# A recurrence that centres v in its transposing product and sums over head channels by one fp32 product

## The chip, the core and the metric

The kernel runs on one core of one Trainium2 chip. The metric is the device time of one execution in microseconds; three runs gave 1673.81, 1668.88 and 1673.68 us, with a median of 1673.68. All other times here come from one profiled execution, which took 1675.3 us and whose span from the first to the last instruction is 1673.2 us. Names of engines: PE is TensorE (PEld its weight loads), DVE is VectorE, ACT is ScalarE, POOL is GpSimd, SP is SyncE, whose queue issues most DMAs.

## The reference

One block of a hybrid transformer, with 1024 positions of width 1024: a normalised and modulated input, a token mixer of two branches (attention with forget gates, and an RWKV7 recurrence, each with 8 heads of 64 channels), a gated merge of both, and a feed-forward part with a short convolution. Only the recurrence is changed. Its core, cut to what matters:

```
kk = heads(k * k_k)
kk = kk / jnp.maximum(jnp.sqrt(jnp.sum(kk * kk, axis=-1, keepdims=True)), L2_EPS)
...
def step(state, inp):
    r_t, w_t, k_t, v_t, a_t, b_t = inp
    sa = jnp.einsum('bhvk,bhk->bhv', state, a_t)
    state = state * w_t[:, :, None, :] + sa[..., None] * b_t[:, :, None, :] + v_t[..., None] * k_t[:, :, None, :]
    y_t = jnp.einsum('bhvk,bhk->bhv', state, r_t)
    return state, y_t
...
mean = jnp.mean(y, axis=-1, keepdims=True)
var = jnp.mean(jnp.square(y - mean), axis=-1, keepdims=True)
y = ((y - mean) * lax.rsqrt(var + GN_EPS)).reshape(bsz, seq, RWKV_WIDTH) * ln_w + ln_b
bonus = (jnp.sum(r_h * k_h * r_k, axis=-1, keepdims=True) * v_h).reshape(bsz, seq, RWKV_WIDTH)
return ((y + bonus) * g).astype(p.dtype)
```

Four sums run over the 64 channels of a head: of kk squared, of r k r_k, of y (its mean) and of the squared, centred y (its variance). Since y is linear in v along the channels of v, a v whose mean over these channels is zero gives a y whose mean is zero.

## The kernel before

The kernel works channel-major: the 128 partitions hold the channels of two heads, the free axis 512 positions. Large products are made of three fp32r products each (high x high, high x low and low x high halves of the operands), 24 matrix products of 128x512 for one output tile of a 1024-deep contraction.

Stages of the profiled execution: modulation and start (0 to about 55 us), the first projections and the lora chain (to 149), the recurrence (149 to 627), attention (627 to 839), the branch products br (839 to about 905), and the output product and feed-forward part (to the end).

The recurrence goes through eight units (p, hf): a pair of heads p (0 to 3) and a half hf of the positions, in the order (0,0), (0,1), (1,0) and so on. For each unit

- `pre` makes ssq (the sum of kk squared), decays, keys and scores, transposes v and a scaled a to position-major tiles vt and at (4 transposes each, copied to UV by ACT and to QA by DVE), transposes keys (tb), forms q from scores and UV, the sum bs and with it bon, the bonus, on DVE;
- `inverse` inverts triangular 32x32 blocks on DVE, by 62 small instructions (t and E, L740 and L744 before, L732 and L736 after); the result E goes through DRAM (DMAs se, then TT) into TT;
- `main` transposes TT to X on DVE (L881), and TensorE makes from X and TT in turn xi, zi and uw, and then eight chunks of sp and yp, where sp updates the state S (L941) and yp is the output. The rest of `main` takes y from PSUM, subtracts its mean, divides by its deviation, applies ln_w, ln_b and the bonus, and stores o.

The next unit's `pre` runs beside a unit's `main`. Before the change a helper, `head_sums`, makes each sum over head channels: ACT casts the operand to fp32r (hi), POOL subtracts (lo), and TensorE multiplies both by blk_r, a matrix of two 64x64 blocks of ones.

What sets the order: TensorE's order is written out by a planner, `Weave`. Each chain of work is a generator; `weave.now` advances by the planned cost of each product (`mm_cost`), a chain yields the planned nanoseconds until it can go on, and in between the planner takes single products from a queue of large ones: r, k, v and q, k projections (ps_rkv, qk), the position-major v, and at last 16 gates (gt; 48 products each). What is left of the queue when the recurrence ends is used up in attention, where a gate runs in one PSUM buffer, rk_ps, as a late gate: 24 products for a half, then Abs and Relu on ACT read rk_ps, then Exp, Ln, an addition on DVE, Exp and a store to d_gate (`gate_out`, L1186). `drain` ends attention only when no gate is pending. Behind it `br_open` casts and splits the first weights of the branch products (hi_br, L1242). In the recurrence the other engines' orders come from a scheduler; in attention DVE's and ACT's are the order of the code.

Attention's heads are loaded by POOL's queue (`load_head`: stA, stB, vh), and SP's queue issues the stores of the gates.

## Time and profile before

| what | from where | value |
|---|---|---|
| time | median of three runs | 1673.68 us |
| profiled execution | its own time; its span | 1675.3 us; 1673.2 us |
| granted TensorE clock | mean over the span | 0.986 |
| recurrence, 149 to 627 us | PE, DVE, ACT, POOL busy | 472.75, 348.22, 215.57, 62.98 us |
| attention, 627 to 839 us | PE, DVE, ACT, POOL busy | 199.57, 163.32, 140.16, 50.43 us |
| sums over head channels | POOL subtractions L727, four groups of eight | 11.7 + 11.4 + 10.4 + 10.4 us |
| granted clock of attention | mean, 627 to 839 us | 0.97 |

How to read it: busy times of several engines overlap, so they are not added; an engine that is busy for nearly the whole of a stage sets that stage's time. In the rows shown below, a group of instructions has its line, engine, operation, output<-inputs and count, then busy us and the mean ns of one, then the idle time before them with what ended it; a timeline row has start and duration in us; a row of waits has the total, the times and the longest. A row of a window has its length, then busy us of PE, PEld, DVE, ACT and POOL, the granted clock as a share of full speed, the DMA share and GB/s. A matmul's recorded duration contains its way through the array; what one costs in a row of them is the distance from start to start.

### The profile page before, as it was taken

To read this page: it belongs to the slowest core of one execution; us is meant where nothing else is said; L and a number is where in the kernel's file an instruction comes from. 1 tells how busy PE (TensorE), PEld (TensorE's weight loads), DVE (VectorE), ACT (ScalarE), POOL (GpSimd) and SP (SyncE) were. 2 spreads that over 40 slices of the span, in tenths; PEclk is the share of its full clock that TensorE was granted. 3 is DMA by queue.
4 is the path that set the end of the run, shared out by engine and by line. 5 is a ranking of instruction groups with operands and counts; after the bars stand their busy time and mean duration, and the time that the engine had idled before them with its cause. 6 is when DMAs were issued, how large, how long until landed. Compare 5 with 4: busy or idle time off the path is not lost.

```text
span 1673.2 us, 26056 instructions
## 1 busy us (share of the span) xinstructions
PE 1622.3 (97%) x9772; PEld 1333.2 (80%) x9772; DVE 1227.8 (73%) x2390; ACT 808.3 (48%) x1482; POOL 147.8 (9%) x175
## 2 busy tenths in 40 slices
PE   5899999999999998999999999999999999999998
PEld 4677877787977777888878888888888888888886
DVE  5786787888876635888778445897777777786677
ACT  5453343434455545767623244654444444455455
POOL 0010101111111012322022000000000000000000
PEclk8899999999999999999999999999999999999999
DMA  8497744433343236433197420143223323574463
GB/s 333 133 327 213 194 124 130 129 102 113 96 127 92 80 112 155 127 113 119 36 344 264 164 89 39 63 131 108 102 95 99 116 95 108 190 274 154 129 210 107
DMA packets 120974, 239.85 MB, mean 143 GB/s; under 512 B 39888, under 2 KB 48336, under 8 KB 120848
## 3 DMA queue, kind: packets, MB, share of 16 engines
q1 hardware_dynamic: 112896, 220.94, 40.8%
q0 software_dynamic: 7952, 17.25, 3.9%
q8 instruction: 77, 1.26, 0.3%
q14 instruction: 49, 0.40, 0.1%
HBM read 172.59 MB, written 65.54 MB: 142 GB/s over the span
## 4 chain that ended last, share of the span: by engine, by line
PE 82%; DVE 9%; DMA 4%; ACT 3%; issue 2%; SPq 1%; POOL 0%; DVEq 0%; ACTq 0%
PE X L144 13%; PE D L144 13%; PE Y L144 6%; PE gt L144 6%; PE ps_rkv L144 6%; PE wo L144 5%; PE br L144 5%; PE rk_ps L144 4%; PE W L144 3%; PE v L144 2%; PE lg L144 2%; PE ov L144 2%; PE tp L151 2%; PE qk L144 2%; PE low L144 1%
## 5 line engine op out<-in xcount | busy, mean ns | idle before, releaser
L144 PE MATMUL D<-op,op 128*128 128x512 f32 x924 | 209.8, 389 | 0.0
L144 PEld LDWEIGHTS D<-op,op 128*128 128x128 f32 x924 | 173.3, 188 | 36.3 <-DVE op L1269 0.3
L144 PE MATMUL X<-T_m,S 128*128 128x512 f32 x440 | 107.2, 390 | 0.1
L144 PEld LDWEIGHTS X<-T_m,S 128*128 128x128 f32 x440 | 82.4, 188 | 18.2 <-ACT T_m L1694 0.5
L1268 ACT CAST op<-g 128x512 fp32r<-128x512 f32 x77 | 47.8, 621 | 73.8 <-PE D L144 47.9
L1269 DVE TENSOR_TENSOR op<-g,op 128x512 fp32r<-128x512 f32 x77 | 53.0, 688 | 41.5 <-ACT op L1268 41.5
L1505 DVE SCALAR_TENSOR_TENSOR c<-ab,vec,c 128x512 f32<-128x512 f32 x88 | 65.8, 749 | 19.5 <-ACT c L1508 17.9
L1469 DVE TENSOR_TENSOR S<-ur,S 128x512 fp32r<-128x512 f32 x66 | 45.5, 691 | 35.9 <-ACT S L1465 35.7
L270 DVE TENSOR_TENSOR lo_in<-raw_in,hi_in 128x512 fp32r<-128x512 f32 x84 | 57.9, 727 | 14.0 <-PE gt L144 5.0
L1465 ACT CAST S<-ur 128x512 fp32r<-128x512 f32 x66 | 41.0, 622 | 55.8 <-DVE ur L1458 30.9
L1469 DVE TENSOR_TENSOR A<-ur,A 128x512 fp32r<-128x512 f32 x64 | 44.0, 687 | 30.9 <-ACT A L1465 30.7
L268 ACT CAST hi_in<-raw_in 128x1024 fp32r<-128x1024 f32 x42 | 43.9, 1048 | 44.4 <-PE ps_rkv L144 26.6
L740 DVE TENSOR_TENSOR t<-E,M 128x60 f32<-128x60 f32 (+24 forms) x248 | 56.0, 226 | 12.0 <-DMA M<-sm 5.7
L144 PE MATMUL Y<-T_h,A 128*128 128x512 f32 x264 | 63.5, 389 | 0.0
L144 PE MATMUL Y<-T_h,S 128*128 128x512 f32 x264 | 63.3, 389 | 0.0
L744 DVE TENSOR_TENSOR E<-E,t 128x60 f32<-128x60 f32 (+24 forms) x248 | 56.8, 229 | 5.8
L144 PE MATMUL X<-B_b,A 128*128 128x512 f32 x252 | 60.8, 390 | 0.0
L144 PE MATMUL W<-B_f,A 128*128 128x512 f32 x252 | 60.6, 389 | 0.0
L1090 ACT ACTIVATE P<-lg,nm 128x896 f32<-128x896 f32 (+3 forms) x64 | 47.4, 743 | 22.8 <-DVE nm L1086 22.6
L144 PEld LDWEIGHTS Y<-T_h,A 128*128 128x128 f32 x264 | 49.5, 188 | 10.4
L144 PEld LDWEIGHTS Y<-T_h,S 128*128 128x128 f32 x264 | 49.5, 188 | 10.3
L1465 ACT CAST A<-ur 128x512 fp32r<-128x512 f32 x64 | 39.8, 623 | 34.1 <-PE X L144 29.4
(473 smaller groups left out, 4151.9 us busy)
## 6 DMA issues: line engine op xcount, KB each, us to landing
raw_in<-in_w_in SPq DMA_DIRECT2D x50, 512.0 KB, 4.3
wm<-in_w_mod SPq DMA_DIRECT2D x48, 512.0 KB, 7.4
ur<-in_w_up SPq DMA_DIRECT2D x44, 512.0 KB, 4.3
g<-d_g SPq DMA_DIRECT2D x35, 512.0 KB, 3.9
d_g<-gs SPq DMA_DIRECT2D x44, 256.0 KB, 2.0
d_g<-c SPq DMA_DIRECT2D x33, 256.0 KB, 4.6
d_st<-qh SPq DMA_DIRECT2D x64, 128.0 KB, 2.4
d_gate<-gs SPq DMA_DIRECT2D x32, 256.0 KB, 2.7
```

The costliest lines, as they stand in the source:

```text
L144: weave.last = nc.tensor.matmul(o, lhsT, rhs, start=start, stop=stop, skip_group_check=more)
L151: nc.tensor.transpose(o, i, eye)
L268: nc.scalar.copy(hi, raw)
L270: nc.vector.tensor_tensor(lo[:, c : c + NH], raw[:, c : c + NH], f32(hi[:, c : c + NH]), op=ALU.subtract)
L740: i = tt(tv, E32[:, 0:J, s : s + 1].to_broadcast([128, J, W]), M32[:, s : s + 1, s + 1 : 32].to_broadcast([128, J, W]), op=ALU.mult)
L744: tt(E32[:, 0:J, s + 1 : 32], E32[:, 0:J, s + 1 : 32], tv, op=ALU.add)
L1090: nc.scalar.activation(e[:, 0:n], lg[:, 0:n], AF.Exp, bias=nm[:, 0:1], accum_out=nm[:, 1:2])
L1268: nc.scalar.copy(hi, src)
L1269: tt(lo, src, f32(hi), op=ALU.subtract)
L1465: nc.scalar.copy(hi, src)
L1469: tt(lo, src, f32(hi), op=ALU.subtract)
L1505: stt(c, ab[:, x + hf * NH : x + hf * NH + NH], V("conv_w", 22 * x + i), c, op0=ALU.mult, op1=ALU.add)
```

## The change

The sums ssq, bs and va become one fp32 product each with the fp32 matrix blk, read directly from the constants: no cast, no subtraction, no fp32r halves. The sum mu and the subtraction of the mean from y (L959) go. Instead a matrix cen = I - blk/64 is made once, and vt is the product of v with cen (four fp32 128x128 products for four transposes), so UV holds a v that is centred over the head channels; bon still reads v itself. Square reads y directly from PSUM. The planned waits change: ahead of ssq 1275 (6000 in the first unit) and 3400 become 3000 (9000), ahead of bs 3400 becomes nothing, at the end of `main` 700, 3400, 2700 and 3400 become 1300. The planner's cost of an fp32 product of over 256 columns is halved.

```diff
-            self.now += n / 0.6
+            self.now += n / 1.2
...
-        blk_r = rw.tile([128, 128], F32R, name="blk_r")
-        nc.scalar.copy(blk_r, C("blk"))
-
-        def head_sums(ps, x, hi, lo):
-
-            nc.scalar.copy(hi, x)
-            nc.gpsimd.tensor_tensor(lo, x, f32(hi), op=ALU.subtract)
-            yield 3400
-            mm(ps, blk_r, hi, start=True, stop=False)
-            mm(ps, blk_r, lo, start=False, stop=True)
+        cen = rw.tile([128, 128], F32, name="cen")
+        stt(cen, C("blk"), -1.0 / CH, ident, op0=ALU.mult, op1=ALU.add)
...
-            yield 1275 if p + hf else 6000
+            yield 3000 if p + hf else 9000
             ssq = gen(f"ssq{n}")
-            yield from head_sums(ssq, ksq, parts[:, 0, :], parts[:, 1, :])
+            mm(ssq, C("blk"), ksq, start=True, stop=True)
...
-                transpose(vt[:, bs], vv[:, bs], ident)
+                mm(vt[:, bs], vv[:, bs], cen, start=True, stop=True)
...
-            yield from head_sums(bp, rkb, tmp("cum", dt=F32R), tmp("en", dt=F32R))
+            mm(bp, C("blk"), rkb, start=True, stop=True)
...
+            yf = yp.rearrange("p c s -> p (c s)")
+            ysq = rw.tile([128, NH], F32, tag="ysq", name=f"ysq{n}", bufs=1)
+            nc.scalar.activation(ysq, yf, AF.Square)
             y = rw.tile([128, NH], F32, tag="y", name=f"y{n}", bufs=1)
-            nc.scalar.copy(y, yp.rearrange("p c s -> p (c s)"))
...
-            yield 700
-            yield from head_sums(mu, y, part("Zt", "r"), part("Mt", "r"))
-            stt(y, mu, -1.0 / CH, y, op0=ALU.mult, op1=ALU.add)
-            ysq = rw.tile([128, NH], F32, tag="ysq", name=f"ysq{n}", bufs=1)
-            nc.scalar.activation(ysq, y, AF.Square)
-            yield 2700
+            nc.scalar.copy(y, yf)
+            yield 1300
             va = gen(f"va{n}")
-            yield from head_sums(va, ysq, part("Zt", "s"), part("Mt", "s"))
+            mm(va, C("blk"), ysq, start=True, stop=True)
```

The change moves work in the orders. Over the whole program 48 gate products that ran in the recurrence as gt (432 before, 384 after) run in attention as rk_ps (336 before, 384 after). Three places:

DVE in the recurrence, ahead of the X of unit (1,0), before (E32, t32 and M32 with 1_0 belong to the inverse of that unit, names with 1_1 to the `pre` of the next, lo_in22 and k20 to a projection that fills TensorE):

```order
L740 TENSOR_TENSOR t321_0_2653<-E321_0_2651,M321_0_2519 128x8
L744 TENSOR_TENSOR E321_0_2651<-E321_0_2651,t321_0_2653 128x8
L823 TENSOR_TENSOR E1_1_3046<-p1_1_100_3049,cst2_120 128x4x128
L823 TENSOR_TENSOR E1_1_3046<-p1_1_110_3050,cst2_120 128x4x128
L270 TENSOR_TENSOR lo_in22_3074<-raw_in22_3071,hi_in22_3073 128x512 x2
L365 SCALAR_TENSOR_TENSOR k20_2753<-ps_rkv60_2997,omu_80,sh_rkv60_3066 128x512
L359 MEMSET sh_rkv100_3379 128x1
L959 SCALAR_TENSOR_TENSOR y0_1_3043<-mu0_1_3045,y0_1_3043 128x512
L823 TENSOR_TENSOR E1_1_3046<-p1_1_104_3100,cst2_120 128x4x128
L823 TENSOR_TENSOR E1_1_3046<-p1_1_114_3101,cst2_120 128x4x128
L270 TENSOR_TENSOR lo_v00_3134<-raw_v00_3131,hi_v00_3133 128x512 x2
L881 STREAM_TRANSPOSE X1_0_3200<-TT1_0_2524 32x256 x2
```

and the same place after:

```order
L736 TENSOR_TENSOR E321_0_2707<-E321_0_2707,t321_0_2709 128x8x3
L270 TENSOR_TENSOR lo_in22_3081<-raw_in22_3078,hi_in22_3080 128x512 x2
L732 TENSOR_TENSOR t321_0_2709<-E321_0_2707,M321_0_2560 128x16
L365 SCALAR_TENSOR_TENSOR k20_2705<-ps_rkv60_3007,omu_80,sh_rkv60_3073 128x512
L736 TENSOR_TENSOR E321_0_2707<-E321_0_2707,t321_0_2709 128x8x2
L359 MEMSET sh_rkv100_3215 128x1
L732 TENSOR_TENSOR t321_0_2709<-E321_0_2707,M321_0_2560 128x8
L736 TENSOR_TENSOR E321_0_2707<-E321_0_2707,t321_0_2709 128x8
L853 COPY QA1_1_2971<-q1_1_3120 128x8x64
L857 TENSOR_TENSOR bon1_1_3140<-bs1_1_3138,v11_1891 128x512
L872 STREAM_TRANSPOSE X1_0_2954<-TT1_0_2565 32x256 x2
```

The last instructions of the inverse moved behind lo_in22 and k20, and X moved behind the next unit's QA and bon; in units (2,0) and (3,0) X stands behind bon too.

TensorE at that place of the program, after (unit (1,1)'s q and bs, unit (1,0)'s xi):

```order
L144 MATMUL q1_1_3120<-UV1_1_2972,E1_1_2970 64x64 x16
L144 MATMUL bs1_1_3138<-ksq1_1_2856,cst2_120 128x512
L144 MATMUL xi1_0_3145<-X1_0_2954,E1_0_2403 32x32 x16
L144 MATMUL ps_rkv20_3086<-u_lo_111,hi_in14_3001 128x512 x5
```

Before, xi stood behind q, and bs stood elsewhere; now bs, which bon reads, stands between them.

ACT at the end of attention, before (th casts transposed probabilities, o and fx take the output of the last head, hi_br is the first weight of the next stage):

```order
L1198 ACTIVATE gs_1_9172<-gs_1_9172 128x512
L1157 COPY o_8846<-ov 64x256
L1123 CAST th_21_9208<-tp_21_9198 128x512
L1123 CAST th_22_9211<-tp_22_9204 128x384
L1157 COPY o_8846<-ov 64x256
L1170 CAST fx_6857<-o_8846 128x512
L1242 CAST hi_br_9251<-raw_br_9249 128x512
```

and after:

```order
L1154 CAST fx03_6582<-o31_8599 128x512
L1174 ACTIVATE gs15_0_9018<-rk_ps_6643 128x512
L1175 ACTIVATE gm15_0_9019<-rk_ps_6643 128x512
L1177 ACTIVATE gs15_0_9018<-gs15_0_9018 128x512
L1178 ACTIVATE gs15_0_9018<-gs15_0_9018 128x512
L1182 ACTIVATE gs15_0_9018<-gs15_0_9018 128x512
L1174 ACTIVATE gs15_1_9052<-rk_ps_6643 128x512
L1175 ACTIVATE gm15_1_9053<-rk_ps_6643 128x512
L1177 ACTIVATE gs15_1_9052<-gs15_1_9052 128x512
L1178 ACTIVATE gs15_1_9052<-gs15_1_9052 128x512
L1182 ACTIVATE gs15_1_9052<-gs15_1_9052 128x512
L1226 CAST hi_br00_9079<-raw_br00_9077 128x512
```

Both halves of the last gate now stand between fx and hi_br. TensorE there, after (before, br follows the last ov directly):

```order
L144 MATMUL ov<-tl_22_8996,vh_8378 128x256
L144 MATMUL rk_ps<-u_hi,lo_in_8667 128x512 x7
L144 MATMUL rk_ps<-u_hi,hi_in_8666 128x512 x8
L144 MATMUL rk_ps<-u_lo,hi_in_8666 128x512 x8
L144 MATMUL rk_ps<-u_hi,lo_in_8667 128x512 x8
L144 MATMUL br_00_9125<-fx_6579,hi_br_9079 128x512
```

31 of the last gate's 48 products moved behind the last output product of attention; the other 17 stand among the products ahead of these rows.

POOL between the recurrence and attention, before (stA, stB and vh load one head; hi_in and lo_in split the weights of a late gate):

```order
L1032 DMA stA0_6848<-d_st_94 128x2x1024
L1034 DMA stB0_6850<-d_st_94 68x2x1024
L1036 DMA vh0_6852<-d_v_95 128x1024
L262 CAST hi_in36_6893<-raw_in36_6891 128x1024
L1032 DMA stA1_6966<-d_st_94 128x2x1024
L1034 DMA stB1_6968<-d_st_94 68x2x1024
L1036 DMA vh1_6970<-d_v_95 128x1024
```

and after:

```order
L1016 DMA stA0_6573<-d_st_94 128x2x1024
L1018 DMA stB0_6575<-d_st_94 68x2x1024
L1020 DMA vh0_6577<-d_v_95 128x1024
L1016 DMA stA1_6719<-d_st_94 128x2x1024
L1018 DMA stB1_6721<-d_st_94 68x2x1024
L1020 DMA vh1_6723<-d_v_95 128x1024
L262 CAST hi_in35_6646<-raw_in35_6644 128x1024
```

The loads of the second head moved ahead of the first split, so the first two heads' loads stand together.

More of the change, by code (lines that the diff above doesn't have):

```diff
@@ L776, in pre @@
             nc.scalar.activation(ksq, kk, AF.Square, scale=V("k_k", p))
-            parts = rw.tile([128, 3, NH], F32R, tag="bk", name=f"kp{n}")
-            yield 1275 if p + hf else 6000
+            yield 3000 if p + hf else 9000
             ssq = gen(f"ssq{n}")
-            yield from head_sums(ssq, ksq, parts[:, 0, :], parts[:, 1, :])
+            mm(ssq, C("blk"), ksq, start=True, stop=True)
             behind(nc.vector.tensor_tensor_scan(cum, C("reset"), cum, initial=0.0, op0=ALU.mult, op1=ALU.add))
```

3 lines of the change are left out of this document (removed).

## The prediction

> **What bounds the kernel now.** I read the page's engine shares first, then TensorE's waits and the busy times of the recurrence (149 to 628 us), then the single places that the change touches.
>
> ```profile
> PE 1622.3 (97%) x9772; PEld 1333.2 (80%) x9772; DVE 1227.8 (73%) x2390; ACT 808.3 (48%) x1482; POOL 147.8 (9%) x175
> ```
> ```profile
> 149.00:628.00 479.00, 473.75 (x4366) 382.51 (x4366) 348.83 (x968) 216.20 (x379) 63.98 (x81) 1.00 0.44 122
> ```
> ```profile
> PE qk L144 <- DVE v L365: 2.2, 1, 2.2
> PE sp L144 <- DVE S L941: 1.5, 3, 0.9
> ```
>
> TensorE is busy 97% of the span, and 473.75 of the 479 us of the recurrence. Its two largest waits there come to 2.2 + 1.5 = 3.7 us. So work taken from ACT, POOL and DVE gains nothing by itself in this stage: what counts is TensorE's own work, and whether the new order makes it wait where it did not.
>
> **TensorE's own work.** Prices:
>
> ```profile
> L144 PE MATMUL mpb<-acc,cst x8: 591/592/592, 128.8 to 146.3; 128*128 128x512 f32 x8
> L248 DVE TENSOR_TENSOR gb<-mpb,bb x4: 670/682/692, 131.4 to 146.9; 128x512 f32<-128x512 f32 x4
> ```
> ```profile
> 145.89 0.19 PEld L144 LDWEIGHTS mpb<-acc,cst 128*128 128x128 f32 x1 [0.24 <-issue]
> 146.32 0.19 PEld L144 LDWEIGHTS qk<-u_hi,lo_in 128*128 128x128 f32 x1 [0.24 <-issue]
> ```
> ```profile
> 268.56 0.40 PE L144 MATMUL mu<-Ztr,blk_r 128*128 128x512 f32 x1
> 268.80 0.39 PE L144 MATMUL mu<-Mtr,blk_r 128*128 128x512 f32 x1
> 269.11 0.71 PE L144 MATMUL p<-ar,bk 64*128 64x128 f32 x8
> ```
> ```profile
> 986.96 4.29 PE L144 MATMUL tr<-dg,h_sb 128*128 128x128 f32 x37
> ```
> ```profile
> 176.41 0.27 PE L151 MATMUL vt<-cst,v 128*128 128x128 f32 x1
> 176.52 0.27 PE L151 MATMUL at<-cst,ar 128*128 128x128 f32 x1
> ```
> ```profile
> 627.13 1.98 PE L144 MATMUL rk_ps<-u_hi,hi_in 128*128 128x512 f32 x8
> 628.95 1.98 PE L144 MATMUL rk_ps<-u_lo,hi_in 128*128 128x512 f32 x8
> ```
>
> mpb is a full fp32 product of the size of the new sums. Its four products (four readers gb) leave eight records, and their weight loads follow each other by 0.43 us: two passes, 0.86 us. The pair of fp32r products that it replaces took 268.56 to 269.11, 0.55 us, of which 0.455 is two pitches of (628.95 - 627.13) / 8 = 0.2275 and the rest the edge. With the same edge a new sum costs 0.95. So 24 x 0.95 - 32 x 0.55 = **+5.3 us**: fewer sums, but each is dearer. A 128x128 fp32 pass costs (4.29 - 0.27) / 36 = 0.112, two of them 0.223, against 0.11 for a transpose; 32 products for vt: **+3.6**. The order puts 48 gate products fewer in the recurrence and 48 more behind it: 48 x 0.2275 = **-10.9** here. Sum of the stage: -2.0 us.
>
> What goes elsewhere is large and off the path: 32 casts on ACT, 32 subtractions on POOL, 8 corrections by the mean on DVE. The Square of y now reads PSUM before y is copied; in unit (1,0), say, the order has eight two-pass score products p (16 passes, 1.1 us by the row at 269.11) and five short v products between the last chunk and va, 1.7 us, which cover it if it costs what Exp does (0.63, below). The larger waits in front of ssq leave its Square done long before. I cost these at nothing; uncovered, a sum would wait 0.6 us, 5 us in eight units.
>
> **X behind a late sum.** In units (1,0), (2,0), (3,0) the DVE order now has X (L872) behind bon (L857), which reads bs, and bs stands directly ahead of xi, which reads X. Nothing on TensorE is left to fill this: at the least 0.1 + 0.68 (bon) + 2 x 0.43 (X) + 0.1 = 1.75 us each. The inverse that X needs ends late as well. From its last DVE instruction to X the path leads through two DMAs:
>
> ```profile
> 219.74 0.17 DVE L744 TENSOR_TENSOR E<-E,t 128x8 f32<-128x8 f32 x1
> ...
> 220.43 0.68 DVE L866 TENSOR_TENSOR bon<-bs,v 128x512 f32<-128x512 f32 x1
> 221.03 1.28 DVE L270 TENSOR_TENSOR lo_in<-raw_in,hi_in 128x512 fp32r<-128x512 f32 x2
> ...
> 226.13 0.43 DVE L881 STREAM_TRANSPOSE X<-TT 32x256 f32<-32x256 f32 x1 [3.82 <-DMA TT<-se]
> 226.83 0.44 DVE L881 STREAM_TRANSPOSE X<-TT 32x256 f32<-32x256 f32 x1 [0.27 <-DMA TT<-se]
> ```
> ```profile
> 324.60 0.71 PE L151 MATMUL tb<-cst,bk 64*128 64x64 f32 x16
> 325.36 1.15 PE L144 MATMUL q<-UV,E 64*64 64x64 f32 x32
> 326.44 0.69 PE L144 MATMUL xi<-X,E 32*32 32x32 f32 x32
> ```
>
> ```profile
> 427.61 1.12 PE L144 MATMUL v<-hi_v,u_hi 128*128 128x256 f32 x8
> ```
> ```profile
> L850 DVE COPY QA<-at 64x256 f32<-64x256 f32 x32 | 13.5, 421 | 7.5 <-PE at L151 7.2
> L968 DVE SCALAR_TENSOR_TENSOR y<-y,vec,rs 128x512 f32<-128x512 f32 x8 | 6.0, 752 | 6.8 <-ACT rs L967 6.7
> ```
> ```profile
> L966 ACT ACTIVATE rs<-va,epsr 128x512 f32<-128x512 f32 x8 | 5.5, 684 | 6.6 <-PE va L144 6.6
> L967 ACT ACTIVATE rs<-rs 128x512 f32<-128x512 f32 x8 | 5.0, 631 | 0.3
> ```
>
> 219.91 to 227.27, from the last inverse instruction's end to X's, is 7.4 us. In unit (1,0) the last four inverse instructions stand among lo_in and k, which wait for the end of the k products. Behind these TensorE has 11 products (2.5 us), tb and q (326.44 - 324.60 = 1.84) and bs (0.95), 5.3 us up to xi. DVE needs 1.3 (lo_in), 0.75 (k, priced as y of L968) and 4 x 0.17, 2.6 us less overlap and plus a start, for what is left, so the inverse ends 2.6 before xi is due and xi waits 7.4 - 2.6 = 4.8. In the same way (2,0): 38 short v products at (1.12 - 0.28) / 7 = 0.12 and the 2.8 of tb, q and bs give 7.3 from the at transposes that QA waits for; DVE then has four QA at 0.42 and eight inverse instructions at 0.2, 3.3, so the inverse ends 4.0 ahead and xi waits 3.4. Unit (3,0): 17 products (3.9) and 2.8 give 6.7, less 3.6 (one instruction more, and starts), 3.1, wait 4.3. Together **+12.5**, between 5.3 (only the queue behind bon) and 3 x 7.4 = 22. In unit (1,1) the halves of X stand around y, behind va, Ln and Exp: 0.69 + 0.63, two y at 0.75, 2 x 0.43, vs at 0.42 and starts, some 4.3, against 14 v products, 1.7 us: **+2.5**, between 0 and 4.3. Of the waits of before, the 2.2 for v (behind X, which waited 3.82 for its DMA) should go, since X has more room in unit (0,0): **-2.2**, between 0 and -3.7.
>
> **The clock.**
>
> ```profile
> 712.18 0.69 PE L144 MATMUL ov<-th,vh 128*128 128x256 f32 x2 [2.20 <-DVE o L1159]
> ```
> ```profile
> 637.00:645.00 8.00, 7.62 (x21) 6.07 (x22) 0.69 (x1) 2.10 (x4) 0.79 (x1) 0.60 1.02 212
> 712.00:720.00 8.00, 7.72 (x30) 6.41 (x30) 6.26 (x13) 3.34 (x7) 0.00 (x0) 0.59 0.55 150
> ```
>
> Behind TensorE waits of 4.64 us (quoted below) and of 2.20 the granted clock was 0.60 and 0.59 over 8 us, 3.2 us lost each time; behind the 2.2 for v it stayed 1.00. I take a loss at 1.5 of the three X waits, **+4.8**, and one at the end. The Trainium skill, page "TensorE: Matmul & The Clock Gate", section "Why this matters for your kernels", asks for no idle gap over about 3 us; the trace has a loss behind 2.20 already, so it is stricter here. By that rule all four waits pay, a result of its own below.
>
> **The seam to attention, and its end.**
>
> ```profile
> 636.24 0.60 ACT L1190 ACTIVATE gs<-rk_ps 128x512 f32<-128x512 f32 x1 [5.59 <-DMA d_gate<-gs]
> ...
> 639.26 0.63 ACT L1198 ACTIVATE gs<-gs 128x512 f32<-128x512 f32 x1 [0.76 <-DVE gs L1196]
> ```
> ```profile
> 637.38 3.78 PE L144 MATMUL rk_ps<-u_hi,hi_in 128*128 128x512 f32 x8 [4.64 <-ACT gm L1191]
> ```
> ```profile
> 832.90 0.44 PE L144 MATMUL ov<-th,vh 128*128 128x256 f32 x2 [1.01 <-ACT th L1123]
> ...
> 836.69 0.44 PE L144 MATMUL ov<-tl,vh 128*128 128x128 f32 x2
> 839.21 2.11 PE L144 MATMUL br<-fx,hi_br 128*128 128x512 f32 x8 [2.08 <-ACT hi_br L1242]
> ```
>
> At 632.7 TensorE stops since ACT waits for a gate store that lies beside the loads of attention's first heads. After the change POOL issues these loads together and earlier, so the store may be free: between 0 and -(4.64 + 3.2); I take **-2.0**, nearer to no change, because the stores and loads are as many.
>
> At the end of attention stand the 48 moved products: 17 among the last P V products (3.9 us, 1.0 of it in the idle time at 832.9: +2.9), then 31 (7.05). Between the gate's halves rk_ps is read by Abs and Relu, 1.3 us (637.38 - 636.24 and a start). The ACT order then has the whole gate chain ahead of hi_br: 639.89 - 636.24 = 3.65, a cast of 0.62, starts 0.2: 4.5 us in which TensorE has nothing. Against this the 2.1 of before goes. 2.9 + 7.05 + 1.3 + 4.5 - 2.1 = **+13.6**, and **+3.2** for the clock. Low end: the products alone, 10.9 - 1.0 - 2.1 = +7.8.
>
> **The sum.** 1675.3 (profiled execution: span 1673.2 and 2.1 around it) - 2.0 + 12.5 + 2.5 - 2.2 + 4.8 - 2.0 + 13.6 + 3.2 = 1705.7. The median shown is 1.6 lower, so **1704 us**, 1.8% slower.
>
> **Rivals.**
>
> - *Inverse in time* (0.22). Only the queue behind bon is paid: 12.5 becomes 5.3, no clock loss there: 1704 - 7.2 - 4.8 = 1692. For it: DVE, 73% busy, gets time back. Where a POOL subtraction runs, a DVE instruction is stretched:
>
> ```profile
> 253.22 1.27 POOL L727 TENSOR_TENSOR en<-ksq,cum 128x512 fp32r<-128x512 f32 x1 [5.96 <-ACT cum L726]
> ```
> ```profile
> 253.37 1.18 DVE L744 TENSOR_TENSOR E<-E,t 128x42 f32<-128x42 f32 x1
> ```
>
>   1.18 where a smaller one above took 0.17: at most 1.0 us in each of 32 subtractions goes with L727. Against it: in the three units DVE waits for products, not for DVE's own work. The Trainium skill, page "GPSIMD Engine Reference", section "1. Specifications", says the same of DVE instructions with two SBUF inputs; by it DVE gains in every unit.
> - *TensorE never waits* (0.16), the side on which it is not slower. Place: X, the seam, the end. It decides where each inverse ends over 7.4 us before xi, and hi_br is cast before the last gate product. Then the time is TensorE's work: +5.3 + 3.6, less 3.7, 4.64 + 3.2 at the seam, and 3.1 of idle (1.0 + 2.1) that gate products fill: -5.7, 1668. For it: that is how the recurrence ran before. Against it: the ACT order puts hi_br last.
> - *Every new wait halves the clock* (0.09): 1.5 x 3.2 more, 1709.
> - *The fp32 sum costs 0.43*, as the changed planner has it (0.03): 24 x 0.43 = 10.3 less, 1694. mpb speaks against it.
>
> **How the numbers follow.** The forecast holds 0.50, with 1696 to 1712 of its own from the bounds above. 1686 to 1713 takes in the late clock, the cheap sum and most of the first rival, and leaves out the second and the tails. A measurement can tell 0.3%, 5 us, from no change. Faster by more: 0.10, the second rival as it stands; within: 0.06, the same with the clock lost once or twice (1671 to 1674); slower: 0.84, all others.
>
> **What would show it.** ssq, bs, va with two records each at a pitch of 0.43; waits of xi for X in (1,0), (2,0), (3,0) of 3 to 5 us, with DVE waiting for TT; the clock near 0.6 behind them; 48 rk_ps products just ahead of br, and a wait for hi_br of 4 to 5 us. If xi waits under 2 us, the inverse step was wrong; if br follows rk_ps at once, the end was.

## The result and the profile after

The changed kernel took a median of 1717.46 us (four runs, 1711.44 to 1718.87) against 1673.74 us for the kernel before: 1.0254 times the time before, 95% interval 1.0238 to 1.0271. It is slower, as forecast, but the time lies 4.5 us above the range, which ended at 1713. The profiled execution took 1711.44 us, with a span of 1709.7 us; the three others are 5.8 to 7.4 us longer.

The page's engine shares and the row of the recurrence, which now lasts to the first rk_ps product at 653.59 us (627.13 before):

```profile
PE 1641.4 (96%) x9788; PEld 1340.3 (78%) x9788; DVE 1209.4 (71%) x2381; ACT 788.7 (46%) x1450; POOL 108.6 (6%) x148
```
```profile
149.00:653.00 504.00, 483.10 (x4331) 381.95 (x4330) 328.65 (x958) 190.86 (x336) 20.59 (x50) 0.98 0.42 115
```

The work went where the change sends it: over the program DVE, ACT and POOL lost 18, 20 and 39 us. But in this stage TensorE, busy for all but 5 us before, now has 21 us without work, and its clock fell to 0.98. TensorE's waits in this stage (total, times, longest):

```profile
PE xi L144 <- DVE X L872: 16.4, 8, 4.7
PE qk L144 <- DVE ql L391: 2.1, 1, 2.1
PE sp L144 <- DVE sh_rkv L359: 2.0, 1, 2.0
```

Before, no wait of xi for X stood among the largest. The timeline of unit (1,0), DVE first, then TensorE:

```profile
326.14 0.17 DVE L736 TENSOR_TENSOR E<-E,t 128x8 f32<-128x8 f32 x1
327.31 0.69 DVE L853 COPY QA<-q 128x512 f32<-128x512 f32 x1 [1.00 <-PE q L144]
328.36 0.69 DVE L857 TENSOR_TENSOR bon<-bs,v 128x512 f32<-128x512 f32 x1 [0.35 <-PE bs L144]
332.49 0.43 DVE L872 STREAM_TRANSPOSE X<-TT 32x256 f32<-32x256 f32 x1 [3.44 <-DMA TT<-se]
333.28 0.43 DVE L872 STREAM_TRANSPOSE X<-TT 32x256 f32<-32x256 f32 x1 [0.36 <-DMA TT<-se]
...
326.12 1.15 PE L144 MATMUL q<-UV,E 64*64 64x64 f32 x32
327.19 1.12 PE L144 MATMUL bs<-ksq,cst 128*128 128x512 f32 x2
333.07 0.28 PE L144 MATMUL xi<-X,E 32*32 32x32 f32 x2 [4.75 <-DVE X L872]
```

From the end of the last inverse instruction (326.31) to the end of X (333.71) pass 7.4 us, as before the change. What changed is that TensorE reaches xi only 2 us behind the inverse's end. DVE is done with bon at 329.05 and then waits 3.44 us for the DMA of TT: the queue behind bon is not what is late, the inverse is.

Windows of the same execution behind the waits of the recurrence, across the seam, and behind br's wait:

```profile
256.00:264.00 8.00, 7.58 (x47) 5.18 (x49) 2.94 (x17) 0.60 (x1) 0.11 (x1) 0.79 0.37 90
333.00:341.00 8.00, 7.51 (x49) 6.05 (x50) 1.07 (x3) 2.46 (x4) 0.00 (x0) 0.58 0.08 20
383.00:391.00 8.00, 7.82 (x109) 7.38 (x110) 2.53 (x5) 1.82 (x5) 0.00 (x0) 0.79 0.30 83
444.00:452.00 8.00, 7.43 (x74) 7.31 (x75) 4.10 (x19) 1.47 (x4) 0.00 (x0) 0.79 0.33 88
569.00:577.00 8.00, 7.17 (x78) 5.62 (x79) 5.91 (x27) 1.04 (x3) 0.00 (x0) 0.61 0.44 126
640.00:700.00 60.00, 56.59 (x313) 47.44 (x313) 33.90 (x64) 36.37 (x78) 19.29 (x24) 1.00 0.61 159
872.00:880.00 8.00, 7.18 (x19) 5.65 (x20) 1.63 (x3) 1.28 (x3) 2.51 (x2) 0.57 0.82 263
```

The granted clock is the third column from the right. The five rows of the recurrence each lose (1 - clock) x 8 us, 11.5 us together. The seam to attention, and attention's end (TensorE, then ACT):

```profile
662.28 1.90 PE L144 MATMUL rk_ps<-u_hi,hi_in 128*128 128x512 f32 x7 [3.09 <-ACT gm L1175]
...
862.83 2.11 PE L144 MATMUL rk_ps<-u_hi,hi_in 128*128 128x512 f32 x8 [1.18 <-ACT gm L1175]
872.82 3.78 PE L144 MATMUL br<-fx,hi_br 128*128 128x512 f32 x8 [4.25 <-ACT hi_br L1226]
...
868.61 0.60 ACT L1174 ACTIVATE gs<-rk_ps 128x512 f32<-128x512 f32 x1 [3.26 <-PE rk_ps L144]
871.62 0.63 ACT L1182 ACTIVATE gs<-gs 128x512 f32<-128x512 f32 x1 [0.76 <-DVE gs L1180]
872.16 1.12 ACT L1226 CAST hi_br<-raw_br 128x512 fp32r<-128x512 f32 x2
```

The seam's wait fell from 4.64 to 3.09 us without a clock loss behind it. At the end the last gate's 24 products of its second half run alone, and br waits 4.25 us behind ACT's gate chain. The new sums, by the groups of the recurrence:

```profile
L144 PE MATMUL vt<-cen,v 128*128 128x128 f32 x64 | 11.4, 279 | 0.0
L144 PE MATMUL bs<-ksq,cst 128*128 128x512 f32 x16 | 9.0, 645 | 0.0
L144 PE MATMUL va<-ysq,cst 128*128 128x512 f32 x16 | 8.2, 591 | 0.0
```

Eight sums bs leave sixteen records, as mpb did, and eight times four products vt leave 64.

### The profile page after: what moved, and what is told of

It reads as the page before. It is cut to its first block, busy times and chain, and to the rows that moved or that the text cites. A ratio compares the mean times of both kernels' runs of the same rounds, so it can differ in the third digit from the quotient of the medians.

```text
span 1709.7 us, 26032 instructions
## 1 busy us (share of the span) xinstructions
PE 1641.4 (96%) x9788; PEld 1340.3 (78%) x9788; DVE 1209.4 (71%) x2381; ACT 788.7 (46%) x1450; POOL 108.6 (6%) x148
## 4 chain that ended last, share of the span: by engine, by line
PE 83%; DVE 8%; DMA 4%; ACT 2%; issue 1%; SPq 1%; DVEq 0%; ACTq 0%
PE X L144 13%; PE D L144 12%; PE Y L144 6%; PE ps_rkv L144 6%; PE br L144 5%; PE wo L144 5%; PE qk L144 5%; PE gt L144 5%; PE rk_ps L144 4%; PE W L144 3%; PE lg L144 2%; PE ov L144 2%; PE v L144 2%; PE tp L151 2%; PE sp L144 1%
## 5 line engine op out<-in xcount | busy, mean ns | idle before, releaser
L270 DVE TENSOR_TENSOR lo_in<-raw_in,hi_in 128x512 fp32r<-128x512 f32 x82 | 53.1, 688 | 23.0 <-PE ps_rkv L144 12.6
L732 DVE TENSOR_TENSOR t<-E,M 128x60 f32<-128x60 f32 (+24 forms) x248 | 51.8, 209 | 17.3 <-DMA M<-sm 11.4
L736 DVE TENSOR_TENSOR E<-E,t 128x60 f32<-128x60 f32 (+24 forms) x248 | 51.5, 208 | 5.5
```

The lines of the kernel that those rows point to most:

```text
L270: nc.vector.tensor_tensor(lo[:, c : c + NH], raw[:, c : c + NH], f32(hi[:, c : c + NH]), op=ALU.subtract)
L732: i = tt(tv, E32[:, 0:J, s : s + 1].to_broadcast([128, J, W]), M32[:, s : s + 1, s + 1 : 32].to_broadcast([128, J, W]), op=ALU.mult)
L736: tt(E32[:, 0:J, s + 1 : 32], E32[:, 0:J, s + 1 : 32], tv, op=ALU.add)
```

## Experiments: is it the place of bs, the gate, the centring or the sums?

All ratios are to the kernel before, run on the same chip, with 95% intervals. Milestones in profiled executions are the first rk_ps product (627.13 before, 653.59 after) and the distance from there to the first br (212.08 and 219.23).

**bs_wait** gives back bs its planned wait:

```diff
             bp = gen(f"bs{n}")
+            yield 3400
             mm(bp, C("blk"), rkb, start=True, stop=True)
```

> The changed kernel, only the planned wait of 3400 between q and bs put back, so that bon no longer stands directly ahead of X. Theory (late X, and the clock it costs): the waits of xi fall from 16.4 us to 5 to 8, since in unit (3,0) and (1,1) X is free and in (1,0) and (2,0) only QA or a projection's eviction stands ahead of it; two of the clock losses of the recurrence go with them, 3 to 7 us; together 11 to 17 us less than the changed kernel: 1700 to 1706 us. Rival (the fp32 products are dearer than the trace of before showed): waits go, but the time stays at 1712 or above.

1702.71 us, ratio 1.0185 (1.0163 to 1.0207). The time is in the range, the reason is not: bs and bon went behind X in unit (1,0), the wait of xi there grew, and all waits of xi together came to 11.4 us, not 5 to 8.

```profile
323.20 0.17 DVE L736 TENSOR_TENSOR E<-E,t 128x8 f32<-128x8 f32 x1
330.38 0.43 DVE L873 STREAM_TRANSPOSE X<-TT 32x256 f32<-32x256 f32 x1 [4.49 <-DMA TT<-se]
...
330.96 0.28 PE L144 MATMUL xi<-X,E 32*32 32x32 f32 x2 [6.14 <-DVE X L873]
```

These are rows of its timeline, DVE and then TensorE. With no bon ahead of X, but with tb, q and bs now behind xi on TensorE too, xi waits 6.14 us. X waits for its DMA, and xi stands too early in the order.

**gate_back** uses the last gate up before attention:

```diff
-    while len(weave.queue) > 12:
+    while len(weave.queue) > 6:
```

> The changed kernel, with one gate more taken from the queue before attention starts, so that the 48 products stand ahead of attention as before the change (432 and 336 instead of 384 and 384). Theory (the moved gate costs 11.9 us ahead of br and 2.9 us of clock behind it, and saved 10.9 in the recurrence): the end of attention is 14.8 us shorter, the stretch before attention 10.9 longer, so 4 us faster than the changed kernel, 1713, br directly behind the last output product with a wait near 2 us; if the stall at the start of attention comes back too, 1717. Rival (the moved gate is the larger part of the loss): 10 us or more faster, below 1708.

1705.2 us, ratio 1.0197 (1.0174 to 1.0220). Br follows 208.37 us behind the first rk_ps, which itself comes 11.1 us later: the products moved, and br's wait went back to 2.08 us. It gained 12 us in the medians, which is the rival's side (10 us or more), not the theory's 4. Not all of that is the gate: in the profiled executions, of which the changed kernel's was its shortest, the gain is 2.6 us.

**cen_only** is the kernel before with the centred v alone: cen in vt, no mu, and with it planned waits of 700 instead of 700 + 3400 + 2700 between yp and the sum va. **sums_only** is the kernel before with each pair of fp32r products replaced by one fp32 product; planned waits and mu stay.

```diff
...
-                transpose(vt[:, bs], vv[:, bs], ident)
+                mm(vt[:, bs], vv[:, bs], cen, start=True, stop=True)
...
-            yield 700
-            yield from head_sums(mu, y, part("Zt", "r"), part("Mt", "r"))
-            stt(y, mu, -1.0 / CH, y, op0=ALU.mult, op1=ALU.add)
...
-            yield 2700
+            yield 700
```
```diff
-            nc.scalar.copy(hi, x)
-            nc.gpsimd.tensor_tensor(lo, x, f32(hi), op=ALU.subtract)
             yield 3400
-            mm(ps, blk_r, hi, start=True, stop=False)
-            mm(ps, blk_r, lo, start=False, stop=True)
+            mm(ps, C("blk"), x, start=True, stop=True)
```

> The kernel before, with v centred by the transposing product and the mean sum left out; the other sums stay pairs of fp32r products with their old waits, except one planned wait of 700 behind Square. cen is written over the constant blk, which only made the fp32r matrix. Theory: TensorE does 3.6 us more for vt and 4.4 less for the eight mean sums; xi of unit (1,0) waits about 2 us; 1672 to 1678 us. Rival (vt itself is the cost: its 64 passes or the reads of cen disturb the recurrence): 1685 or above.

> The kernel before, with each of the 32 sums (the mean's too) as one fp32 product and without casts and subtractions, all planned waits and the planner's old cost kept. Theory (a sum costs 0.95 instead of 0.55 us): TensorE does 32 x 0.4 = 12.8 us more in the recurrence, minus what DVE gains by the POOL work that goes (nothing, since TensorE is the bound): 1684 to 1690 us, and ssq, bs, mu, va each leave two records at a pitch of 0.43. Rival (POOL's subtractions slow DVE, so their end repays it): 1670 to 1677 us.

cen_only took 1704.75 us, ratio 1.0200 (1.0180 to 1.0220): a clear miss, and the turning point of the study. It has the old sums, on their old engines, and its largest waits on TensorE in the recurrence are X's:

```profile
PE xi L144 <- DVE X L884: 15.7, 6, 8.0
```

sums_only took 1680.53 us, ratio 1.0055 (1.0034 to 1.0076), without such waits and below its range. Its first rk_ps came 10.1 us later; the sum had said 32 x (0.95 - 0.55) = 12.8. So neither the fp32 sums nor the order of bs makes X late. What the slow kernels share is the shorter planned tail of `main`: 700 + 3400 + 2700 + 3400 = 10200 planned ns before, 1300 in the changed kernel, 4100 in cen_only.

## Experiments: the planner's estimate of X

`pre` writes down when X will be there, 38500 planned ns after it sends the blocks to be inverted (47500 in the first unit), and `main` waits until 1500 before that:

```
            ready = weave.now + (47500 if k == 0 else 38500)
...
            yield max(0, o["ready"] - weave.now - 1500)
```

The new theory: with a long tail of the unit before, the next `main` came later than this estimate anyway, so that nobody noticed that it is some 4 us too early; with the short tail the estimate decides. It foretells that a later estimate (**ready_late**) or the old tail (**tail_back**), each a single number in the changed kernel, removes the waits, and that the halved cost of fp32 products in the planner (**old_cost**) does not matter.

```diff
-            ready = weave.now + (47500 if k == 0 else 38500)
+            ready = weave.now + (47500 if k == 0 else 44500)
```
```diff
             nc.scalar.copy(y, yf)
-            yield 1300
+            yield 10200
```
```diff
-            self.now += n / 1.2
+            self.now += n / 0.6
```

> The changed kernel, only the planner's estimate of when a unit's inverse is ready moved from 38500 to 44500 planned ns behind the scores. Theory (in the kernel before, the planned waits of the mean and variance sums, 10200 ns at the end of each unit, kept the next unit's xi away from its inverse; with 1300 in their place the estimate 38500 decides, and it is too early by about 4 us): the order puts 432 gate products back in front of attention, all waits of xi fall below 1 us together, the granted clock of the recurrence is 1.00 apart from at most one loss, br waits about 2 us. The recurrence then has 472 + 10.9 us of TensorE work and about 5 of waits: 20 to 28 us less than the changed kernel on the same chip, 1685 to 1693. Rival (the centred v or the fp32 sums hold up xi in another way, or cost more than thought): less than 12 us gained, 1700 or above.

> The changed kernel, only the planned wait ahead of va at the end of a unit put back from 1300 to 10200 ns (the sum of the waits before the change). Theory (that wait was what gave the inverse its time): the waits of xi vanish as with the later estimate; 480 gate products in front of attention; 1683 to 1693 us. Rival (bs directly ahead of xi is the cause): waits of 3 to 5 us stay in units (1,0), (2,0) and (3,0), 1705 or above.

> The changed kernel, only the planner's cost of a 512 wide fp32 product put back to n / 0.6 (853 ns, near the 860 measured). The order has 384 gate products in front of attention as with the change, and X behind bon in units (1,0), (2,0), (3,0); in unit (1,1) X no longer stands among the two y. Theory (the shortened wait at the end of a unit and the estimate of readiness make X late, not the halved cost): waits of xi of 10 to 14 us, within 6 us of the changed kernel, 1708 to 1718. Rival (the halved cost misplaces the work): below 1703.

| kernel | us | ratio (95%) | first rk_ps | to br |
|---|---|---|---|---|
| ready_late | 1689.55 | 1.0094 (1.0071 to 1.0116) | 639.92 | 207.49 |
| tail_back | 1688.01 | 1.0088 (1.0068 to 1.0107) | 648.53 | 200.28 |
| old_cost | 1718.43 | 1.0262 (1.0245 to 1.0278) | 653.47 | 226.76 |
| changed_again | 1716.93 | 1.0249 (1.0223 to 1.0275) | 652.21 | 225.91 |

changed_again is the unedited changed kernel, run on the same chip as ready_late, tail_back and busy; old_cost and head_later come from another chip, where the kernel before took 1673.89 us against 1673.68.

> The changed kernel once more, on the same chip as the others of this group, as their yardstick and for its spread: 1709 to 1719 us. Theory of the clock: executions differ by one to three losses of 1.7 to 3.4 us behind the same waits, so the profiled clock and the span go together, 0.001 of the clock for some 1.7 us; rival: the waits themselves differ by several us.

ready_late and tail_back came in their ranges. old_cost lies 0.4 us above its own, within 2 us of changed_again as the theory said, but its waits of xi grew to 21.3 us where 10 to 14 were expected. TensorE's waits in the recurrence with the old tail:

```profile
PE sp L144 <- DVE S L932: 1.9, 3, 1.2
PE qk L144 <- DVE ql L391: 1.8, 1, 1.8
PE sp L144 <- DVE sh_rkv L359: 0.9, 1, 0.9
```

No xi is left in it. Nor is br's long wait: the longer plan uses up more of the queue, so that 480 gate products run ahead of attention (432 with the later estimate, 384 in the changed kernel). One planned number thus carried both the X waits and the gate at attention's end: 29 of the 43 us.

## Experiments: the clock and the seam

**busy** issues four products that nobody reads (blk times the constant reset, into xi's own PSUM tile) ahead of xi in units (1,0), (1,1), (2,0) and (3,0), unseen by the planner. X comes no earlier, but TensorE isn't idle.

```diff
             xi = gen(f"xi{n}")
+            if n in ("1_0", "1_1", "2_0", "3_0"):
+                t0 = weave.now
+                for _ in range(4):
+                    mm(xi, C("blk"), C("reset"), start=True, stop=True)
+                weave.now = t0
```

> The changed kernel with four fp32 products of constants (4 x 0.86 = 3.4 us), whose results are overwritten, put on TensorE directly ahead of xi in units (1,0), (1,1), (2,0), (3,0), the units in which xi waits 3.5 to 5.2 us. The waits stay, TensorE is busy in them. Theory (the clock loss follows from TensorE's idling): no loss behind these four, so 8 to 10 us less than the changed kernel, with xi starting at about the same times. Rival (the loss does not hang on the idling there, or costs little): within 3 us of the changed kernel; if the products are not hidden, up to 8 us slower.

1712.25 us, ratio 1.0234 (1.0217 to 1.0251), with six runs from 1699.02 to 1715.19: 4.7 us less than changed_again, between the theory's 8 to 10 and the rival's 3. The profiled execution, 1699.02, reached rk_ps at 641.47 us, 12.1 before the changed kernel, and this is its clock from 150 to 640 us:

```profile
150.00:640.00 490.00, 483.48 (x4340) 376.96 (x4339) 326.88 (x955) 190.58 (x335) 19.90 (x50) 1.00 0.41 115
```

In this execution the losses behind the X waits are gone. The 12.1 us hold some 3 us more that have another source: from 0 to 149 us its clock was 0.93, the changed kernel's 0.91. Four of the other five runs gained only 2 to 5 us against 1716.93. They have no trace, but their recorded mean clocks are 0.980 to 0.984, against 0.988 and 0.986 in the two short ones: the clock makes up some 14 of the 16 us between the shortest and the longest. Where it was lost there is not known, so that unread products keep the clock up is shown in one execution, not for the kernel.

**head_later** puts the three loads of the second head behind the first late gate:

```diff
-        nc.gpsimd.dma_start(A, d_st[h, 0:2, :, :].rearrange("k r s -> r k s"))
+        i = nc.gpsimd.dma_start(A, d_st[h, 0:2, :, :].rearrange("k r s -> r k s"))
+        if h == 1:
+            behind(i)
...
+        if h == 1:
+            behind(j)
+            behind(i)
```

> The changed kernel, only the three loads of attention's second head ordered on POOL behind the split of the late gate's weights, so that the gate stores at the start of attention lie beside one head's loads (2.1 MB) instead of two (4.1 MB). Theory (stall at the start of attention of 3.1 us in one execution and 7.9 in another, ACT waiting for a gate store that shares the DMA engines with the loads): the stall falls below 2.5 us and so does its variation; 3 to 8 us less than the changed kernel, 1708 to 1713. Rival (the stall comes from ACT's or SP's order): the stall stays at 3 us or more, 1714 to 1718; or the second head comes late and attention waits.

1704.69 us, ratio 1.0190 (1.0177 to 1.0204): 12 us less than changed_again, more than expected. The seam of changed_again explains most of it (ACT, then TensorE):

```profile
664.56 0.60 ACT L1174 ACTIVATE gs<-rk_ps 128x512 f32<-128x512 f32 x1 [6.76 <-DMA d_gate<-gs]
...
665.70 3.78 PE L144 MATMUL rk_ps<-u_hi,hi_in 128*128 128x512 f32 x8 [7.88 <-ACT gm L1175]
```

and in head_later:

```profile
655.30 2.11 PE L144 MATMUL rk_ps<-u_hi,hi_in 128*128 128x512 f32 x8 [1.18 <-ACT gm L1180]
```

The first profiled execution of the changed kernel had 3.09 us here and was 5.7 us shorter. gs is written again only when a store to d_gate has left it, and these two rows show how much that wait varies. Whether the seam makes the spread of the other executions, which have no trace, is not shown.

## Experiments: does centring cost anything by itself?

**cen_ready** is cen_only with the estimate 44500, **cen_ready_head** also has head_later's edit.

> The kernel before with v centred by the product, without mean sums, the other sums as pairs of fp32r products (the group cen_only), and the planner's estimate of readiness at 44500 instead of 38500. Theory (late X was the whole loss of the centred v; TensorE's work is 3.6 - 4.4 us): the waits of xi vanish, recurrence within 4 us of the kernel before, 1669 to 1678 us in all. Rival (the centred v has a price of its own): 1685 or above.

> cen_ready with the loads of the second head behind the split of the late gate's weights. Theory: as cen_ready, with a stall at the start of attention below 2.5 us instead of about 4.6 and no clock loss behind it: 2 to 7 us faster than cen_ready, 1664 to 1672, perhaps faster than the kernel before. Rival: no gain over cen_ready.

1685.18 us, ratio 1.0060 (1.0048 to 1.0073), and 1683.88 us, ratio 1.0057 (1.0045 to 1.0069). Both missed, on their rivals' side. The later estimate took 20 us from cen_only, yet X still comes late in unit (1,0), where xi waits 2.68 + 0.51 us in cen_ready. Either 44500 is not enough there or centring costs something. **cen_tail** decides it: cen_only with the one wait of 700 made 6800, so that 10200 remain in all. **cen_tail_head** adds head_later's edit; **before_head** is the kernel before with head_later's edit alone, and **tail_head** is tail_back with it.

> The kernel before with the centred v (cen in vt, no mu, no subtraction of the mean) and the old paired sums, but with the planned waits at the end of main kept at 10200 in all (700 + 3400 + 2700 become one wait of 6800 ahead of va's 3400). If the removed planned waits are the cause: no wait of xi for X over 1 us, the first rk_ps product at 627 to 631 us, and 1671 to 1678 us, since 32 dearer vt products (+3.6) stand against 16 mean products less (-4.4). Rival, centring costs by itself (a later inverse whatever the plan, as in the kernel with the later estimate of X): xi waits of 2 us and more stay, 1681 to 1688 us.

> Centred v with the planned waits kept at 10200, old paired sums, and the loads of the second head behind the first late gate. If both effects add: the sum of the two, 1664 to 1672 us, the fastest kernel of the study. Rival, they don't add: 1673 to 1680 us.

> The kernel before with only the loads of the second head put behind the first late gate. If the store's wait beside the loads sets the seam: the wait of 4.64 us falls to 1 to 2.5 us and the clock loss of 3.2 behind it goes, 1665 to 1671 us. Rival, POOL's splits or the heads' loads are late instead: 1672 to 1680 us.

> The changed kernel with the planned waits of 10200 at the end of main, and the loads of the second head behind the first late gate. If tail and loads are two separate causes: TensorE's wait at the seam under 2.5 us with no clock loss behind it, and 4 to 8 us less than with the tail alone (1688.0): 1680 to 1684 us. Rival, the seam moves on to another store or load: 1685 to 1690 us.

| kernel | us | ratio (95%) | first rk_ps | to br | seam's wait |
|---|---|---|---|---|---|
| cen_tail | 1673.57 | 0.9997 (0.9987 to 1.0006) | 631.99 | 204.80 | 1.18 |
| cen_tail_head | 1672.91 | 0.9987 (0.9976 to 0.9997) | 628.43 | 207.49 | 1.18 and 1.20 |
| before_head | 1667.89 | 0.9959 (0.9944 to 0.9973) | 625.31 | 205.90 | 2.13 |
| tail_head | 1689.57 | 1.0092 (1.0075 to 1.0108) | 651.11 | 200.09 | 1.18 |

cen_tail and before_head came in their ranges; cen_tail_head lies 0.9 us above its own, and tail_head missed, on its rival's side. With the planned tail kept, the centred v comes out even with the kernel before in the whole time: the recurrence is 4.9 us longer, and attention, whose seam waits 1.18 us instead of 4.64, gives that back. X in unit (1,0) is there 6.5 us ahead of its use, by these rows of the timeline (DVE, then TensorE):

```profile
321.91 0.89 DVE L884 STREAM_TRANSPOSE X<-TT 32x256 f32<-32x256 f32 x2
...
329.35 0.69 PE L144 MATMUL xi<-X,E 32*32 32x32 f32 x32
```

So 33 us of cen_only were the plan. With the seam eased in both, though, centring is 5 us behind (1672.91 against 1667.89). In the profiles the recurrence is 3.1 us longer, with 3.2 us of waits more, attention 1.6 and the stages behind br 1.6. In each of the three TensorE ran at half speed for one stretch of 3.41 us more, 1.7 us lost each time, so that the clock and the waits, not the products, make the difference there. before_head is the fastest kernel, 0.41% under the kernel before: its seam waits 2.13 us and the clock stays at 1.00 (a row of the timeline and one of the windows).

```profile
633.04 2.11 PE L144 MATMUL rk_ps<-u_hi,hi_in 128*128 128x512 f32 x8 [2.13 <-ACT gm L1196]
...
633.00:641.00 8.00, 7.84 (x35) 6.27 (x36) 3.09 (x4) 3.04 (x6) 1.12 (x2) 1.00 1.10 230
```

tail_head gained nothing over tail_back, whose seam waited only 1.18 us already: the old plan alone had eased it.

## Why the prediction was wrong

The direction, the places and most sizes were right. Its sum, against the profiled execution's span of 1709.7 (1673.2 + 36.5):

| term | predicted | measured |
|---|---|---|
| TensorE's work, recurrence | -2.0 | -1.2 (the rest of the stage's +26.5) |
| X, four units | +12.5 + 2.5 | +16.4 (4.75 + 0.42; 3.25 + 0.42; 3.87 + 0.21; in (1,1) 2.35 + 1.13) |
| waits of before | -2.2 | -0.2 (all gaps of over 0.15 us: 4.7 to 4.5) |
| clock, recurrence | +4.8 | +11.5 |
| seam | -2.0 | -4.75 (1.55 of wait, 3.2 of clock) |
| clock in mid attention | not priced | -1.6 (0.79 over 8 us, 0.59 before) |
| end of attention | +13.6 | +13.5 (rest of the +7.15 to br) |
| clock behind br | +3.2 | +2.9 |

- **The step that failed is the clock.** "I take a loss at 1.5 of the three X waits, +4.8" became five losses: behind all four X waits and behind the new wait of 2.0 us for sh_rkv. It cost 11.5 us, 6.7 more than the term had; the sum missed the profiled span by 6.1, and the other errors nearly cancel. The rival "every new wait halves the clock", at 1709, came nearest and was given 0.09. The error was to count units (1,0), (2,0) and (3,0) alone as candidates and to halve their number on the word of one wait of 2.2 us that had no loss; the last section shows why that wait is no guide.
- **The median was taken 1.6 us under the profiled execution**, as it was before. After, it is 6.0 above. The one other profiled execution, changed_again, met a long seam (7.88, with the clock at 0.94 from 640 to 700 us) where this one met a short one (3.09); that the rest did too is not shown, though their mean clocks (0.977 and 0.978, against 0.980) go with it. The step "I take -2.0" at the seam has its sign reversed in changed_again: with two heads' loads issued together the wait grew to 7.88 from the 4.64 of before, and with the second head's put off it is 1.18. Together 6.1 + 7.6 is the distance from 1704 to 1717.5, but for 0.2.
- **X behind a late sum** was right in size (15.0 against 16.4) and in its price of 7.4 us from inverse to X. Its name was wrong: the floor of 1.75 us "behind bon" plays no part, as the first timeline shows (bon done at 329.05, X at 332.49) and bs_wait too. The text named the planned waits in the change but gave them no price; they are the cause, as tail_back and cen_tail show.
- **"The waits of before should go"** failed in kind: the wait for v went, and one of 2.1 us for ql and one of 2.0 for sh_rkv took its place.
- **TensorE's work** was right. Two records for each sum, 64 for vt, and 48 gate products moved. tail_back, with the waits of before and nearly its clock, shows it plainly: its first rk_ps comes 21.4 us later, of which 48 x 0.2275 = 10.9 are the gate products that it moves forward, so 10.5 against 5.3 + 3.6 = 8.9 forecast.
- **The end of attention** went as described, row by row, and in its size. Ahead of it, behind the same kind of wait before ov as in the prediction's row at 712 us, the clock now lost 1.6 us less, which nobody forecast:

```profile
735.00:743.00 8.00, 7.45 (x39) 6.57 (x39) 6.09 (x12) 3.94 (x8) 0.00 (x0) 0.79 0.48 134
```

  gate_back and tail_back undo the moved gate.
- **Inverse in time and TensorE never waits**: tail_back and ready_late reach this state in the recurrence, and come to 1688, not 1668. tail_back's profile is 11.3 us over the kernel before. The dearer products put 10.5 us on its recurrence, and the gate products that it takes out of attention bring only part of their time there: with 288 of them instead of 336 attention's own waits, the seam left out, come to 12.2 us instead of 7.4.

What stays open: where the longer executions of busy lose their clock; whether the long seam is what most executions of the changed kernel meet; and whether an estimate of over 44500 suits the changed kernel better, which was not tried. The 1.6 us by which the stages behind br are longer in most kernels (835.6 against 834.0) are the clock's: up to the last 9 us of the program TensorE ran at half speed there for 3.41 us in all in the four profiles at about 834.0, and for 6.83 us in all in each one at about 835.6.

## What to carry to other kernels

A planned wait is part of the schedule even when the work that it stood for is gone: when a step is removed, ask which later instruction was in time only because of that wait, and set that one's own estimate from the trace (here 38500 planned ns for an inverse that needed some 4 us more). Count each new TensorE wait of about 2 us and more as paid twice, once as idle time and once in the clock, unless the trace shows otherwise at that place: in the 18 profiles of this case all 25 waits of 3.8 us and more, from 149 us to 20 us before the end, were followed by half speed, and 47 of the 67 between 2.0 and 3.8. A resource at the edge of the change, such as a store beside large loads, can decide more than the terms that one computes: look at several executions of it before taking its sign.

## What the runs showed of the hardware

- The clock losses come in two sizes: 0.79 over 8 us (1.7 us) and 0.57 to 0.61 (3.1 to 3.4 us). Below 3.8 us the length of the wait doesn't order them: 2.0 us for sh_rkv cost 1.7, 3.09 at the seam cost nothing, 2.20 before ov cost 3.3 in the kernel before. The Trainium skill, page "TensorE: Matmul & The Clock Gate", section "Part 1: The HAM clock gate", tells of activity windows of 3413 ns that run freely, and of a clock that is halved behind an idle one. An estimate by that page of the Trainium skill: half speed over one or two windows loses 1.7 or 3.4 us, as measured here, and a free-running window would make the outcome depend on where a wait falls. The same page of the Trainium skill asks for no gap of over about 3 us; here the row at 256 us, behind 2.0 us, shows that shorter gaps pay too.
- Where a wait falls orders them better than its length. Within one execution the half-speed stretches begin at whole multiples of 3.413 us from each other (in the changed kernel at 257.73, 332.82, 384.02, 445.46 and 568.34 us). In the kernel before one such boundary, at 227.04 us, splits the wait of 2.23 us for v, so that both intervals are two thirds busy (first two rows), and the clock stays; the wait of 2.20 us before ov lies mostly in the one interval up to 711.74, busy for 1.48 us, and half speed follows (last two rows):

```profile
223.62:227.03 3.41, 2.26 (x10) 1.53 (x9) 0.63 (x2) 0.60 (x1) 0.52 (x2) 1.00 0.54 117
227.04:230.45 3.41, 2.34 (x39) 1.75 (x40) 2.74 (x12) 0.00 (x0) 0.00 (x0) 1.00 0.82 256
708.33:711.73 3.40, 1.48 (x6) 0.86 (x5) 3.37 (x2) 3.40 (x9) 3.12 (x5) 1.00 0.87 285
711.74:718.56 6.82, 6.28 (x18) 5.03 (x19) 6.52 (x13) 3.60 (x7) 0.00 (x0) 0.50 0.60 157
```

  In the 18 profiles, from 149 us to 10 us before the end, each interval of this grid in which TensorE was busy for less than 0.44 of it was followed by half speed, so an interval need not be idle throughout; between 0.44 and 0.70 some were, and above that none, but for one in each profile that lies over 32 products mps of 128x1. Another execution of one kernel can so lose more behind shorter waits: in changed_again xi waited 2.33 and 2.53 us in units (1,1) and (2,0), against 2.35 and 3.25 in the first profile, and half speed lasted 6.83 us behind each instead of 3.41.
- One profiled execution of cen_tail shows a mean clock of 0.938, and its time, 1674.21 us, is that of nine others at 0.983 to 0.986 (1672.67 to 1677.24): a recorded clock that is lower throughout need not mean a longer run.
- A gate store of 256 KB beside the first heads' loads landed 9.7 us after its issue in the changed kernel (of the five issued between 630 and 670 us, the one whose landing the trace has), against a median of 2.5 for the recorded landings of the whole program; the rows of the DMA issues have the count, the KB and the us to landing:

```profile
d_gate<-gs SPq DMA_DIRECT2D x5, 256.0 KB, 9.7
...
d_gate<-gs SPq DMA_DIRECT2D x32, 256.0 KB, 2.5
```

- Without POOL's subtractions the 496 small instructions of the inverse became shorter on DVE, 226 and 229 ns before,

```profile
L744 DVE TENSOR_TENSOR E<-E,t 128x60 f32<-128x60 f32 (+24 forms) x248 | 56.8, 229 | 5.8
```

  208 and 209 after, some 9 us of DVE time in all (sums_only, without these subtractions, has 209 for both; cen_only, with them, 231 and 223):

```profile
L736 DVE TENSOR_TENSOR E<-E,t 128x60 f32<-128x60 f32 (+24 forms) x248 | 51.5, 208 | 5.5
```

  In unit (1,0) this gained nothing behind the inverse, where DVE waits for a DMA.
